# One step behind each chunk: splitting the attention rows inside a tuned streaming-encoder kernel

## The chip, the cores and the metric

The kernel runs on one core of a Trainium2 chip. The metric is device time in microseconds; a kernel's time is the median of several executions. One further execution was recorded by the hardware profiler, and every row of a profile in this text comes from such a recorded execution. The engines are TensorE (PE, with its weight loads listed apart as PEld), VectorE (DVE), ScalarE (ACT), GpSimd (POOL) and SyncE (SP), whose queue issues the transfers (DMA).

## The reference

The reference is one inference step of a one-layer hybrid encoder with 1024 prompt frames and 32 frames of a running stream. Two branches (gated linear attention and differential attention) each produce rows `y`, which are normalised, gated and projected; the two projections are gated again, added, projected by `w_out` and normalised.

```python
def out_merge(x, o_gla, o_diff, gg, dg, ma, mb, gla_norm_g, diff_subln_g, lambda_init,
              w_proj_gla, w_proj_diff, w_out, post_norm_g):
    yg = rmsnorm(o_gla, gla_norm_g).reshape(B, T, GLA_VAL) * jax.nn.silu(gg)
    yd = (rmsnorm(o_diff, diff_subln_g) * (1.0 - lambda_init)).reshape(B, T, DIFF_VAL) * jax.nn.silu(dg)
    merged = jax.nn.sigmoid(ma) * (yg @ w_proj_gla) + jax.nn.sigmoid(mb) * (yd @ w_proj_diff)
    return x + rmsnorm(merged @ w_out, post_norm_g)
```

All is float32. The kernel holds each matrix as a high part, rounded for TensorE, and a low part, what the rounding left; a product is three matmuls (high by high, low by high, high by low).

## The kernel before

The kernel goes through input projections with both attention branches interleaved, then the merge, which is what matters here. Everything is kept transposed: 8 tiles of 128 features by 1056 frames (1024 + 32). The merge has these parts:

1. **First product**, `yg @ w_proj_gla`, in 8 blocks j = 0 to 7 of 128 output features. Each block runs over 3 chunks of 352 frames, and each chunk is 8 x 3 = 24 matmuls into one PSUM bank (`ps_w`, L517 to L519; blocks 0 and 1 are written apart, L1172 to L1174). Two banks take turns. When a chunk is done, DVE evacuates it: one instruction multiplies it with the gate `tha` (L1155). After a block, `done()` stores the gated block to DRAM (`ptd`, L1188) and loads the gate of block j + 2 (L1151).
2. **Rows of the second kind**, `yd`. The 8 row tiles of the differential branch lie in DRAM without their rms scale. For each k: load the row (`ydr`, L1220; two buffers by parity of k), multiply it on DVE by its scale (L1229; the scales of a pair of rows lie in one tile `rsb`, broadcast to all partitions by a 1 MB load, L1225, one buffer), copy the high part on ACT (L1230) into `Y`, subtract on DVE to get the low part (L1231). Then the row buffer is free and row k + 2 is loaded. After an odd row the scale tile of the next pair is loaded.
3. **Second product**, `yd @ w_proj_diff`, with the same chunks and banks (L493 to L495). Its evacuation (L1250) gates a chunk with `thb`, then adds the stored first product `ptl` (L1251) and splits the sum into `m` (L1252 on ACT, L1253 on DVE).
4. **Output product** with `w_out`, whose 4 parts are loaded (`cwr`, L1262) and split as well (`cwh` on ACT, L1270; `cwl` on DVE, L1271). The first part uses the buffers that the rows had: `cwr` those of the even rows, `cwl` those of the odd ones, `cwh` that of the scale tiles.

For every block, the weights are loaded (`wr`, L481), rounded on ACT (`wh`, L483) and split on POOL (`wl`, L485) one block ahead.

In the stage of the change, PE and DVE run in the order in which the code is written (`manual_schedule`), so that DVE does nothing ahead of what stands before it. The orders of ACT and SP are made by a scheduler, and each engine keeps its own strictly. Row splitting stands in `done()` of blocks 3 to 7 (`BESIDE = range(3, KT)`, L40), hence behind all three evacuations of a block; `split_yd` does a whole row. Over blocks 3 to 7 it takes rows 0; 1, 2; 3; 4, 5; 6, 7.

Of the kernel before, what the change touches and what calls it, by code (L numbers as in the profile page):

```python
# [11 lines left out]
F32 = mybir.dt.float32  # L12
# [3 lines left out]
ALU = mybir.AluOpType  # L16
# [9 lines left out]
KT = D // P  # L26
# [13 lines left out]
BESIDE = range(3, KT)  # L40
# [90 lines left out]
def hybrid_step_kernel(ctx: ExitStack, tc: tile.TileContext, a):  # L131
# [3 lines left out]
    ve = nc.vector  # L135
# [3 lines left out]
    def pool(name, bufs=1, **kw):  # L139
        return tc.alloc_tile_pool(name=name, bufs=bufs, **kw)  # L140
# [20 lines left out]
    def bank(name):  # L161
        return bank_of("pj", name)
# [316 lines left out]
    def wtile(b):  # L479
        wr = wp.tile([P, KT, P], F32, tag="wr", bufs=1, name="wr")  # L480
        dma(wr, a["w128"][b])  # L481
        wh = odd(wp, KT, P, tag="wh", name="wh")
        act(wh, wr, AF.Copy)  # L483
        wl = odd(wp, KT, P, tag="wl", name="wl")
        nc.gpsimd.tensor_tensor(wl, wr, wh.bitcast(F32), op=ALU.subtract)  # L485
        return wh, wl
# [11 lines left out]
    def fill(jobs, src, then=None):  # L498

        w = wtile(jobs[0][0])  # L500
        for ji, (b, event, begin, needs) in enumerate(jobs):
            wh, wl = w
            evac = done = None
            for t0, n in CHUNKS:
                ps = None
                for k in range(KT):
                    if k % N["fill"] == 0:
                        yield 0.45 * N["fill"], (needs if ps is None else []), (["pj"] if ps is None else [])
                        if evac is None:
                            if ji + 1 < len(jobs):  # L510
                                w = wtile(jobs[ji + 1][0])
                            elif then is not None:
                                ahead.append(wtile(then))
                            evac, done = begin()
                        if ps is None:
                            ps = bank("ps_w")
                    mm(ps[:, :n], wh[:, k, :], src[k][:, 0, t0 : t0 + n], start=(k == 0), stop=False)  # L517
                    mm(ps[:, :n], wl[:, k, :], src[k][:, 0, t0 : t0 + n], start=False, stop=False)  # L518
                    mm(ps[:, :n], wh[:, k, :], src[k][:, 1, t0 : t0 + n], start=False, stop=(k == KT - 1))  # L519
                with tc.high_priority(offset=N["evac"]):  # L520
                    evac(ps[:, :n], slice(t0, t0 + n))
                S.free("pj", W["w_pj"])
            done()
            S.mark(event)

    ahead = []

    def silu_into(dst):

# [291 lines left out]
    with tc.manual_schedule(engines=PE):  # L821
        left = S.run([[gla_thread(), None, first], [prep_thread(), None, nullcontext],
                      [fill(jobs, xs), None, nullcontext]],
                     until=lambda: ("on", GH - 1, 1) in S.at and jobs[-1][1] in S.at)
# [306 lines left out]
    with tc.manual_schedule(engines=PE):  # L1131
        left = S.run(left + [[diff_main(), None, first], [sample_thread(), None, nullcontext],
                             [fill(jobs, xs, BLK_PG), None, nullcontext]],
                     until=lambda: ("pv", DH - 1, 3) in S.at and jobs[-1][1] in S.at)
# [13 lines left out]
    def load_tha(j):  # L1148
        if j < KT:
            tha[j] = ld("tha")  # L1150
            dma(tha[j], thd[0, j])  # L1151

    def pg_evac(j):
        def evac(ps, sl):
            ve.scalar_tensor_tensor(tha[j][:, sl], tha[j][:, sl], 1.0, ps, op0=ALU.add, op1=ALU.mult)  # L1155
        return evac

    def pg_first():

        w = [ahead.pop(), wtile(BLK_PG + 1)]  # L1160
        for j in range(2):
            load_tha(j)
        b = []
        for j, k in sorted(((j, k) for j in range(2) for k in range(KT)), key=lambda e: (e[1] + N["lead"] * e[0], e[0])):
            yield 1.36, [(("qk", DH - 1), W["yg0"] + W["yg"] * k)], [] if b else ["pj", "pj", "s", "s"]
            if not b:
                d = [dbank("ps_w") for _ in range(2)]
                b = [bank("ps_w"), bank("ps_w")] + [d[n // 2][:, n % 2 * 512 : n % 2 * 512 + 512] for n in range(4)]
            wh, wl = w[j]
            for n, (t0, cw) in enumerate(CHUNKS):  # L1170
                ps = b[j * 3 + n]
                mm(ps[:, :cw], wh[:, k, :], ytiles[k][:, 0, t0 : t0 + cw], start=(k == 0), stop=False)  # L1172
                mm(ps[:, :cw], wl[:, k, :], ytiles[k][:, 0, t0 : t0 + cw], start=False, stop=False)
                mm(ps[:, :cw], wh[:, k, :], ytiles[k][:, 1, t0 : t0 + cw], start=False, stop=(k == KT - 1))  # L1174
            if k == KT - 1:
                with tc.high_priority(offset=N["evac"]):
                    for n, (t0, cw) in enumerate(CHUNKS):
                        pg_evac(j)(b[j * 3 + n][:, :cw], slice(t0, t0 + cw))
                st(ptd[j], tha[j])
                load_tha(j + 2)  # L1180
                for tag in ("pj", "pj") if j == 0 else ("s", "s"):
                    S.free(tag, W["pg_b"])
        yield from fill([pg_job(j) for j in range(2, KT)], ytiles)

    def pg_job(j):
        def begin():
            def done():
                st(ptd[j], tha[j])  # L1188
                load_tha(j + 2)
                if j >= BESIDE[0]:  # L1190
                    for k in range(KT * (j - BESIDE[0]) // len(BESIDE), KT * (j + 1 - BESIDE[0]) // len(BESIDE)):
                        split_yd(k)
            return pg_evac(j), done
        return BLK_PG + j, ("pg", j), begin, []

# [9 lines left out]
    yd = [Y[k // 6][:, k % 6] for k in range(KT)]  # L1205
# [9 lines left out]
    rsb, ydr = {}, {}  # L1215

    def load_yd(k):
        if k < KT:
            ydr[k] = cp.tile([P, T], F32, tag=("cwr", "cwl")[k % 2], name="ydr")
            dma(ydr[k], ydd[k])  # L1220

    def load_rsb(k):
        if k < KT:
            rsb[k // 2] = cp.tile([P, 2, NP], F32, tag="cwh", name="rsb")
            dma(rsb[k // 2], rsd[k : k + 2, :].unsqueeze(0).to_broadcast([P, 2, NP]))  # L1225

    def split_yd(k):
        r = ydr[k]
        ve.tensor_tensor(r[:, 0:NP], r[:, 0:NP], rsb[k // 2][:, k % 2], op=ALU.mult)  # L1229
        act(yd[k][:, 0, :], r, AF.Copy)  # L1230
        ve.tensor_tensor(yd[k][:, 1, :], r, yd[k][:, 0, :].bitcast(F32), op=ALU.subtract)  # L1231
        if k % 2:
            load_rsb(k + 1)
        load_yd(k + 2)

    load_rsb(0)
    load_yd(0)
# [4 lines left out]
    for j in range(KT):  # L1242
# [6 lines left out]
        def evac(ps, sl, th=th, pt=pt, y=y):  # L1249
            ve.scalar_tensor_tensor(th[:, sl], th[:, sl], 1.0, ps, op0=ALU.add, op1=ALU.mult)  # L1250
            ve.tensor_tensor(pt[:, sl], pt[:, sl], th[:, sl], op=ALU.add)  # L1251
            act(y[:, 0, sl], pt[:, sl], AF.Copy, scale=0.5)  # L1252
            ve.scalar_tensor_tensor(y[:, 1, sl], pt[:, sl], 0.5, y[:, 0, sl].bitcast(F32), op0=ALU.mult, op1=ALU.subtract)  # L1253
# [20 lines left out]
    op = pool("op", reuse_waits="tile")  # L1274
# [51 lines left out]
    for u in range(4):  # L1326
# [5 lines left out]
        else:  # L1332

            raw = []
            for k in (0, 4):
                r = op.tile([P, D], F32, tag="xn", bufs=3, name="raw")
                r = r.rearrange("p (k n) -> p k n", k=4)
# [107 lines left out]
```

## Time and profile before

| what | us |
|---|---|
| median of the timed executions (3, from 1445.06 to 1446.31) | 1445.84 |
| profiled execution | 1439.49 |
| its span, first to last instruction | 1437.7 |
| TensorE busy in the span | 1394.2 |
| DVE busy in the span | 717.0 |

Busy time on TensorE is read with care: matmuls overlap, so a row's duration (0.32 us for 352 columns) is longer than the distance between two starts, and the distance between starts is what counts. In rows in order of time, the first number is the start in us from the beginning of the span, the second the duration; the bracket gives how long the engine was idle before and what ended that.

### The profile page before, as it was taken

Reading aid. Unit: us, or ns where it says so; the run is one execution under the profiler, and the core shown is the slowest. Engines: PE = TensorE matmul, PEld = TensorE weight load, DVE = VectorE, ACT = ScalarE, POOL = GpSimd, SP = SyncE. Lnnn points to the kernel's source line nnn. Section 1 sums busy time; section 2 is a strip of 40 time slices with the busy share of each in tenths; the row PEclk is TensorE's granted clock in tenths of the full one; section 3 lists DMA queues with packets and bytes.
Section 4 is the critical chain, followed back from the end, with each engine's and each line's share of the span. In section 5 each row is a group of like instructions: output and inputs, shape, how many; then the busy total and the mean of one; then the engine's idle time right before and its main releaser. Section 6 shows DMA issues by size and latency. Waiting matters only on the chain.

```text
span 1437.7 us, 22643 instructions
## 1 busy us (share of the span) xinstructions
PE 1394.2 (97%) x9074; PEld 1288.8 (90%) x9074; DVE 717.0 (50%) x1448; ACT 556.6 (39%) x1164; POOL 299.9 (21%) x194
## 2 busy tenths in 40 slices
PE   8999999999999999999999999999999999999997
PEld 7687789889989899998989898989999899899997
DVE  5522005666555342565655555565565424555425
ACT  4523104535344232454444444454554422221321
POOL 1200002222223223222232222222221122122002
PEclk9999999999999999999999999999999999999999
DMA  8422111122222233112221322122232475643434
GB/s 308 163 103 98 46 44 57 44 75 85 84 71 76 74 122 100 61 64 87 72 78 52 92 66 86 54 93 66 78 94 76 146 263 203 242 166 128 161 114 150
DMA packets 65251, 152.42 MB, mean 106 GB/s; under 512 B 9664, under 2 KB 28512, under 8 KB 63728
## 3 DMA queue, kind: packets, MB, share of 16 engines
q1 hardware_dynamic: 64992, 150.60, 31.5%
q8 instruction: 75, 1.23, 0.4%
q14 instruction: 40, 0.33, 0.1%
q10 hardware_dynamic: 144, 0.26, 0.0%
HBM read 108.60 MB, written 40.08 MB: 103 GB/s over the span
## 4 chain that ended last, share of the span: by engine, by line
PE 58%; DVE 5%; ACT 1%; issue 1%; DMA 0%; POOLq 0%; DVEq 0%; ACTq 0%
PE ps_w L517 11%; PE ps_w L518 11%; PE ps_w L519 11%; PE ps_s L944 4%; PE ps_t L1006 2%; PE ps_c L1291 2%; PE ps_c L1293 2%; PE ps_c L1292 2%; PE ps_w L495 2%; PE ps_w L493 2%; PE ps_w L494 2%; PE po L1020 1%; PE po L1021 1%; DVE nm L948 1%; PE po L1019 1%
## 5 line engine op out<-in xcount | busy, mean ns | idle before, releaser
L517 PE MATMUL ps_w<-X,wh 128*128 128x352 f32 x1344 | 449.9, 335 | 0.7 <-ACT vo L308 0.4
L518 PE MATMUL ps_w<-X,wl 128*128 128x352 f32 x1344 | 435.2, 324 | 0.8 <-issue 0.8
L519 PE MATMUL ps_w<-X,wh 128*128 128x352 f32 x1344 | 433.5, 323 | 0.0
L485 POOL TENSOR_TENSOR wl<-wr,wh 128x1024 fp32r<-128x1024 f32 x72 | 177.7, 2469 | 561.8 <-ACT wh L483 497.5
L517 PEld LDWEIGHTS ps_w<-X,wh 128*128 128x128 f32 x1344 | 252.8, 188 | 8.4 <-issue 4.7
L518 PEld LDWEIGHTS ps_w<-X,wl 128*128 128x128 f32 x1344 | 253.2, 188 | 1.1 <-issue 1.1
L519 PEld LDWEIGHTS ps_w<-X,wh 128*128 128x128 f32 x1344 | 252.5, 188 | 0.0
L950 ACT ACTIVATE p<-ps_s,nm 128x256 f32<-128x256 f32 (+7 forms) x128 | 94.5, 740 | 63.0 <-DVE nm L948 60.7
L483 ACT ACTIVATE wh<-wr 128x1024 fp32r<-128x1024 f32 x72 | 76.1, 1056 | 68.0 <-PE ps_w L519 40.8
L328 PE MATMUL ps_v<-wh,X 128*128 128x512 f32 x248 | 98.7, 398 | 0.0
L329 PE MATMUL ps_v<-wh,X 128*128 128x512 f32 x248 | 97.6, 394 | 0.8 <-DVE X L245 0.8
L330 PE MATMUL ps_v<-wl,X 128*128 128x512 f32 x248 | 98.3, 396 | 0.0
L948 DVE TENSOR_REDUCE nm<-ps_s 128x1 f32<-128x256 f32 (+7 forms) x128 | 93.2, 753 | 0.0
L1009 DVE TENSOR_TENSOR al<-ps_t,ah 128x512 fp32r<-128x512 f32 (+2 forms) x96 | 53.2, 554 | 35.6 <-ACT ah L1008 34.3
L1008 ACT ACTIVATE ah<-ps_t 128x512 fp32r<-128x512 f32 (+2 forms) x96 | 47.0, 489 | 60.8 <-PE ps_t L1006 60.3
L495 PE MATMUL ps_w<-Y,wh 128*128 128x352 f32 x192 | 61.9, 324 | 0.8 <-DVE Y L1231 0.7
L493 PE MATMUL ps_w<-Y,wh 128*128 128x352 f32 x192 | 62.0, 324 | 0.5 <-DVE thb L1250 0.5
L494 PE MATMUL ps_w<-Y,wl 128*128 128x352 f32 x192 | 61.8, 324 | 0.0
L308 ACT ACTIVATE vo<-ps_v 128x512 f32<-128x512 f32 x32 | 19.0, 595 | 105.7 <-PE ps_v L330 105.3
L1024 DVE SCALAR_TENSOR_TENSOR osb<-po,gs_half,sg 128x256 f32<-128x256 f32 x32 | 15.5, 483 | 88.3 <-ACT sqo L1023 88.3
L328 PEld LDWEIGHTS ps_v<-wh,X 128*128 128x128 f32 x248 | 46.7, 188 | 12.7 <-issue 1.7
L329 PEld LDWEIGHTS ps_v<-wh,X 128*128 128x128 f32 x248 | 46.7, 188 | 12.5 <-DVE X L245 1.7
(319 smaller groups left out, 2681.1 us busy)
## 6 DMA issues: line engine op xcount, KB each, us to landing
wr<-w SPq DMA_DIRECT2D x72, 512.0 KB
thd<-gate SPq DMA_DIRECT2D x16, 528.0 KB
wr<-wv SPq DMA_DIRECT2D x16, 512.0 KB
xn<-xn SPq DMA_DIRECT2D x12, 512.0 KB
newk<-pair SPq DMA_DIRECT2D x8, 528.0 KB
y<-ygd SPq DMA_DIRECT2D x8, 528.0 KB
tha<-thd SPq DMA_DIRECT2D x8, 528.0 KB
ydr<-ydd SPq DMA_DIRECT2D x8, 528.0 KB
```

The costliest lines, as they stand in the source:

```text
L328: mm(ps, xk[:, 0, t0 : t0 + P], wh[:, k, :], start=(k == 0), stop=False)
L329: mm(ps, xk[:, 1, t0 : t0 + P], wh[:, k, :], start=False, stop=False)
L330: mm(ps, xk[:, 0, t0 : t0 + P], wl[:, k, :], start=False, stop=(k == KT - 1))
L485: nc.gpsimd.tensor_tensor(wl, wr, wh.bitcast(F32), op=ALU.subtract)
L493: mm(ps[:, :n], wh[:, k, :], src[k][:, 0, t0 : t0 + n], start=(k == 0), stop=False)
L494: mm(ps[:, :n], wl[:, k, :], src[k][:, 0, t0 : t0 + n], start=False, stop=False)
L495: mm(ps[:, :n], wh[:, k, :], src[k][:, 1, t0 : t0 + n], start=False, stop=(k == KT - 1))
L517: mm(ps[:, :n], wh[:, k, :], src[k][:, 0, t0 : t0 + n], start=(k == 0), stop=False)
L518: mm(ps[:, :n], wl[:, k, :], src[k][:, 0, t0 : t0 + n], start=False, stop=False)
L519: mm(ps[:, :n], wh[:, k, :], src[k][:, 1, t0 : t0 + n], start=False, stop=(k == KT - 1))
L948: ve.tensor_reduce(nm, ps[:, 0:w], axis=AX.X, op=ALU.max, negate=True)
L950: act(p[:, 0:w], ps[:, 0:w], AF.Exp, bias=nm, accum_out=sums[m])
```

## The change

The row splitting is cut into single steps and moved. `scale_yd(k)` does the DVE multiplication and the ACT copy, and after an odd row the load of the next scale tile. `split_yd(k)` does the DVE subtraction and the load of row k + 2. A list of 15 steps is made: scale 0, split 0, scale 1, split 1, and so on, the fourteenth step holds split 6 and scale 7, the fifteenth split 7. A table `beside` hangs one step on each chunk of blocks 3 to 7, directly behind its evacuation.

```diff
                 S.free("pj", W["w_pj"])
+                if event in beside:
+                    beside[event]()
             done()
             S.mark(event)
 
-    ahead = []
+    ahead, beside = [], {}
...
                 load_tha(j + 2)
-                if j >= BESIDE[0]:
-                    for k in range(KT * (j - BESIDE[0]) // len(BESIDE), KT * (j + 1 - BESIDE[0]) // len(BESIDE)):
-                        split_yd(k)
...
-    def split_yd(k):
+    def scale_yd(k):
         r = ydr[k]
         ve.tensor_tensor(r[:, 0:NP], r[:, 0:NP], rsb[k // 2][:, k % 2], op=ALU.mult)
         act(yd[k][:, 0, :], r, AF.Copy)
-        ve.tensor_tensor(yd[k][:, 1, :], r, yd[k][:, 0, :].bitcast(F32), op=ALU.subtract)
         if k % 2:
             load_rsb(k + 1)
+
+    def split_yd(k):
+        ve.tensor_tensor(yd[k][:, 1, :], ydr[k], yd[k][:, 0, :].bitcast(F32), op=ALU.subtract)
         load_yd(k + 2)
+
+    steps = [f for k in range(KT - 1) for f in ((scale_yd, k), (split_yd, k))]
+    steps = [[f] for f in steps[:-1]] + [[steps[-1], (scale_yd, KT - 1)], [(split_yd, KT - 1)]]
+
+    def beside_chunk():
+        for f, k in steps.pop(0):
+            f(k)
+    beside.update({("pg", j): beside_chunk for j in BESIDE})
```

The changed file has other line numbers: the evacuation is L1157, the scaling L1228, the copy L1229, the split L1234; the loads of rows, scale tiles and gates are L1219, L1224 and L1153, the store L1190.

The order of the instructions on DVE, from the first product's evacuations on (`tha<-tha,ps_w`), before:

```order
L1155 SCALAR_TENSOR_TENSOR tha<-tha,ps_w 128x352 x12
L1229 TENSOR_TENSOR ydr<-ydr,rsb 128x1024
L1231 TENSOR_TENSOR Y_12709<-ydr,Y_12709 128x1056
L1155 SCALAR_TENSOR_TENSOR tha<-tha,ps_w 128x352 x3
L1229 TENSOR_TENSOR ydr<-ydr,rsb 128x1024
L1231 TENSOR_TENSOR Y_12709<-ydr,Y_12709 128x1056
L1229 TENSOR_TENSOR ydr<-ydr,rsb 128x1024
L1231 TENSOR_TENSOR Y_12709<-ydr,Y_12709 128x1056
L1155 SCALAR_TENSOR_TENSOR tha<-tha,ps_w 128x352 x3
```

and in the changed kernel at the same place:

```order
L1157 SCALAR_TENSOR_TENSOR tha<-tha,ps_w 128x352 x10
L1228 TENSOR_TENSOR ydr<-ydr,rsb 128x1024
L1157 SCALAR_TENSOR_TENSOR tha<-tha,ps_w 128x352
L1234 TENSOR_TENSOR Y_12709<-ydr,Y_12709 128x1056
L1157 SCALAR_TENSOR_TENSOR tha<-tha,ps_w 128x352
```

The first scaling moves from behind the twelfth evacuation to behind the tenth, and no two steps on rows stand next to each other; the alternation of the last four rows goes on to the end of block 7.

DVE at the end of block 7 and the beginning of the second product (`thb<-thb,ps_w`), before:

```order
L1155 SCALAR_TENSOR_TENSOR tha<-tha,ps_w 128x352 x3
L1229 TENSOR_TENSOR ydr<-ydr,rsb 128x1024
L1231 TENSOR_TENSOR Y_12710<-ydr,Y_12710 128x1056
L1229 TENSOR_TENSOR ydr<-ydr,rsb 128x1024
L1231 TENSOR_TENSOR Y_12710<-ydr,Y_12710 128x1056
L1250 SCALAR_TENSOR_TENSOR thb<-thb,ps_w 128x352 x2
L1251 TENSOR_TENSOR ptl<-ptl,thb 128x352 x2
L1253 SCALAR_TENSOR_TENSOR m_13198<-ptl,m_13198 128x352 x2
L1271 TENSOR_TENSOR cwl<-cwr,cwh 128x512 x3
```

and in the changed kernel:

```order
L1234 TENSOR_TENSOR Y_12710<-ydr,Y_12710 128x1056
L1228 TENSOR_TENSOR ydr<-ydr,rsb 128x1024
L1157 SCALAR_TENSOR_TENSOR tha<-tha,ps_w 128x352
L1234 TENSOR_TENSOR Y_12710<-ydr,Y_12710 128x1056
L1282 TENSOR_TENSOR cwl<-cwr,cwh 128x512
L1261 SCALAR_TENSOR_TENSOR thb<-thb,ps_w 128x352
L1282 TENSOR_TENSOR cwl<-cwr,cwh 128x512
L1262 TENSOR_TENSOR ptl<-ptl,thb 128x352
L1282 TENSOR_TENSOR cwl<-cwr,cwh 128x512
L1264 SCALAR_TENSOR_TENSOR m_13198<-ptl,m_13198 128x352
```

Only the split of row 7 is left behind the last evacuation of block 7. The splitting of the output weights (`cwl`) now begins ahead of the first evacuation of the second product; before, it stood behind the second.

The order of SP's transfers around the second and third scale tile (`rsb`), before:

```order
L1220 DMA ydr<-ydd 128x1056
L1188 DMA ptd<-tha 128x1056
L1225 DMA rsb<-rsd 128x2048
L1220 DMA ydr<-ydd 128x1056
L1151 DMA tha<-thd 128x1056
L481 DMA wr<-w 128x1024
L1220 DMA ydr<-ydd 128x1056
L1188 DMA ptd<-tha 128x1056
L1225 DMA rsb<-rsd 128x2048
```

and in the changed kernel:

```order
L1190 DMA ptd<-tha 128x1056
L1224 DMA rsb<-rsd 128x2048
L1153 DMA tha<-thd 128x1056
L1219 DMA ydr<-ydd 128x1056
L481 DMA wr<-w 128x1024
L1190 DMA ptd<-tha 128x1056
L1219 DMA ydr<-ydd 128x1056
L481 DMA wr<-w 128x1024
L1153 DMA tha<-thd 128x1056
L1224 DMA rsb<-rsd 128x2048
```

A row load and the weight load `wr` have changed places in block 4, and the third scale tile now follows a weight load and a gate load where it followed a row load and a store.

## The prediction

> **What bounds the kernel now.** I read the page first, then busy time by stage, then the waits of TensorE, then the rows of VectorE (DVE) in order of time around those waits.
>
> ```profile
> PE 1394.2 (97%) x9074; PEld 1288.8 (90%) x9074; DVE 717.0 (50%) x1448; ACT 556.6 (39%) x1164; POOL 299.9 (21%) x194
> ```
>
> TensorE is busy for 97% of the span, so a change can gain only where TensorE stands still or runs slow. The stage the change touches is projection blocks 3 to 7 of the first merge product and the start of the second. By windows (columns: stretch, its length, busy us of PE, PEld, DVE, ACT and POOL with counts, clock, DMA share, GB/s):
>
> ```profile
> 1167.00:1178.60 11.60, 11.60 (x74) 11.60 (x73) 2.00 (x4) 1.06 (x1) 2.43 (x1) 1.00 0.88 289
> 1178.60:1190.20 11.60, 11.60 (x75) 11.60 (x74) 1.56 (x3) 1.06 (x1) 2.40 (x1) 1.00 0.49 170
> 1190.20:1201.80 11.60, 11.60 (x74) 11.60 (x74) 4.86 (x5) 2.15 (x2) 2.77 (x1) 1.00 0.52 186
> 1201.80:1218.00 16.20, 13.16 (x74) 12.87 (x73) 7.23 (x7) 3.24 (x3) 2.73 (x1) 0.89 0.66 231
> 1218.00:1229.60 11.60, 11.60 (x74) 11.60 (x74) 4.86 (x5) 2.15 (x2) 2.77 (x1) 1.00 0.75 277
> 1229.60:1243.00 13.40, 11.89 (x74) 11.60 (x74) 7.25 (x7) 3.24 (x3) 2.40 (x1) 1.00 0.68 247
> 1243.00:1257.00 14.00, 12.75 (x75) 11.59 (x74) 10.78 (x14) 6.37 (x9) 2.77 (x1) 1.00 0.57 222
> 1257.00:1268.40 11.40, 11.40 (x73) 11.40 (x72) 6.54 (x11) 2.49 (x4) 2.77 (x1) 1.00 0.62 234
> ```
>
> A block of 72 matmuls takes 11.6 us when nothing disturbs it (the first three rows are blocks 2, 3 and 4). Blocks 5 and 7 (16.20 and 13.40) take longer with TensorE idle, and so does the start of the second product (14.00); behind it TensorE is full again (last row). In block 5 the clock also falls to 0.89. The DVE rows say why:
>
> ```profile
> 1182.65 0.52 DVE L1155 SCALAR_TENSOR_TENSOR tha<-tha,ps_w 128x352 f32<-128x352 f32 x1 [3.32 <-PE ps_w L519]
> 1190.37 0.52 DVE L1155 SCALAR_TENSOR_TENSOR tha<-tha,ps_w 128x352 f32<-128x352 f32 x1 [3.33 <-PE ps_w L519]
> ...
> 1201.97 0.52 DVE L1155 SCALAR_TENSOR_TENSOR tha<-tha,ps_w 128x352 f32<-128x352 f32 x1 [3.35 <-PE ps_w L519]
> 1202.41 1.22 DVE L1229 TENSOR_TENSOR ydr<-ydr,rsb 128x1024 f32<-128x1024 f32 x1
> 1204.78 2.23 DVE L1231 TENSOR_TENSOR Y<-ydr,Y 128x1056 fp32r<-128x1056 f32 x1 [1.16 <-ACT Y L1230]
> 1208.56 1.23 DVE L1229 TENSOR_TENSOR ydr<-ydr,rsb 128x1024 f32<-128x1024 f32 x1 [1.55 <-DMA rsb<-rsd]
> 1210.93 1.26 DVE L1231 TENSOR_TENSOR Y<-ydr,Y 128x1056 fp32r<-128x1056 f32 x1 [1.15 <-ACT Y L1230]
> 1212.11 0.95 DVE L1155 SCALAR_TENSOR_TENSOR tha<-tha,ps_w 128x352 f32<-128x352 f32 x2
> ...
> 1237.21 1.26 DVE L1231 TENSOR_TENSOR Y<-ydr,Y 128x1056 fp32r<-128x1056 f32 x1 [1.15 <-ACT Y L1230]
> 1238.39 0.95 DVE L1155 SCALAR_TENSOR_TENSOR tha<-tha,ps_w 128x352 f32<-128x352 f32 x2
> 1243.12 0.52 DVE L1155 SCALAR_TENSOR_TENSOR tha<-tha,ps_w 128x352 f32<-128x352 f32 x1 [3.78 <-PE ps_w L519]
> ...
> 1250.47 1.26 DVE L1231 TENSOR_TENSOR Y<-ydr,Y 128x1056 fp32r<-128x1056 f32 x1 [1.15 <-ACT Y L1230]
> ...
> 1264.70 0.52 DVE L1250 SCALAR_TENSOR_TENSOR thb<-thb,ps_w 128x352 f32<-128x352 f32 x1 [2.95 <-PE ps_w L495]
> ```
>
> The first two rows evacuate chunks 0 and 2 of block 3: 7.72 us for two chunks, 3.86 us each. Number the 15 chunks of blocks 3 to 7 from 0, and let e(i) be when evacuation i would start undisturbed: e(i) = 1182.65 + 3.86 i. After chunk 5 (1201.97) DVE runs two whole rows back to back, waits in the middle for a new scale tile, and comes to evacuate chunk 6 only at 1212.11, where e(6) = 1205.81. There are two banks for these chunks, so chunk 8 can't start before it:
>
> ```profile
> 1209.32 0.32 PE L519 MATMUL ps_w<-y,wh 128*128 128x352 f32 x1
> 1212.67 0.66 PE L517 MATMUL ps_w<-y,wh 128*128 128x352 f32 x1 [3.04 <-DVE tha L1155]
> 1213.14 0.49 PE L518 MATMUL ps_w<-y,wl 128*128 128x352 f32 x1
> ...
> 1215.73 0.32 PE L518 MATMUL ps_w<-y,wl 128*128 128x352 f32 x1
> ...
> 1237.13 0.32 PE L519 MATMUL ps_w<-y,wh 128*128 128x352 f32 x1
> 1238.96 0.43 PE L517 MATMUL ps_w<-y,wh 128*128 128x352 f32 x1 [1.51 <-DVE tha L1155]
> ```
>
> **The loss, summed.** Matmuls start every 3.86/24 = 0.161 us. The first stop costs 1212.67 - 1209.32 - 0.16 = 3.19. Then ten intervals up to 1215.73 take 3.06 instead of 1.61: 1.45 lost to the lower clock. The stop after chunk 11 costs 1.83 - 0.16 = 1.67 and 0.1 at its restart. Together 6.4. The evacuations confirm it: chunk 14 starts at 1243.12 against e(14) = 1236.69, 6.43 late. The start of the second product loses more: its fifth evacuation (1264.70) is e(19) = 1255.99, so 8.71 late in all, 2.28 of it new. That is where rows 6 and 7 are split only after chunk 14; the last split starts at 1250.47, while the first chunks of the product already want it.
>
> **The change part by part.** No arithmetic is added or taken away: 8 scalings, 8 copies, 8 splits stay. They are spread as one DVE step behind each of the 15 evacuations, and the first comes two chunks earlier.
>
> DVE's load per chunk: an evacuation holds DVE 0.44 (1202.41 - 1201.97), a scaling 1.22, a split 1.26, or 2.23 when it runs beside POOL's work on the next weights, as the rows above show for both. The ScalarE copy, for which a split waited 1.16 each time, now lies in the remainder of the chunk before. A chunk thus holds DVE for 1.7 to 2.7 of 3.86 us. The fullest is chunk 13 (split 6 and scaling 7): 0.44 + 1.26 + 1.22 = 2.9, at most 3.9 beside POOL. Evacuation i may start 3.3 late before TensorE feels it, since chunk i+2 starts at about e(i+1). No stop remains in blocks 3 to 7: gain 6.4. If the cover (the idle DVE of each chunk) were gone, the price would be the late microseconds beyond 3.3.
>
> What must arrive in time are transfers, since each load is issued behind a step and the SyncE (SP) queue is in order:
>
> ```profile
> 1203.65 4.88 DMA rsb<-rsd
> ```
> ```profile
> 1202.52 0.32 SPq L1188 DMA_DIRECT2D ptd<-tha  x1
> 1203.65 0.32 SPq L1225 DMA_DIRECT2D rsb<-rsd  x1
> ...
> 1247.10 0.33 SPq L481 DMA_DIRECT2D wr<-w  x1
> 1247.48 0.42 SPq L1244 DMA_DIRECT2D thb<-thd  x1
> 1248.21 10.39 SPq L1262 DMA_DIRECT2D cwr<-wout  x2
> ```
>
> A scale tile (1 MB) landed 4.88 us after issue, with a store of 528 KB issued 1.1 us ahead. Now it is issued after an odd scaling at e(2n) + 1.7 and wanted two chunks later at e(2n+2) + 0.44, 6.4 us on: hidden, with 1.5 to spare. The third scale tile has a weight load and a gate load just ahead of it (the order of SP, above) in place of a row load and a store, which may take up much of that. If late, DVE may wait 5.5 us more before TensorE does (scaling, 0.44 of evacuation and a hand-over before e(i+2)), so TensorE is safe to 11.9 us. Lower bound of the loss here 0, upper bound 1: I take 0. A row tile (528 KB) has 9.3 us between its issue and its use, row 7 at least 6.7. The weight loads now stand behind row loads that wait for a split, up to 2.7 us later than before; those weights are only needed a block (11.6) after ScalarE could take them, of which its 1.06 and POOL's 2.4 to 2.8 are used. DMA as a whole: the windows of blocks 3 to 7 move about 14.4 MB in 64.4 us, 223 GB/s; in 58 us it is 248, below the 289 of the quiet first window.
>
> At the second product split 7 follows evacuation 14 at e(14) + 0.44 and ends by e(14) + 2.7; its first use is the last matmuls of chunk 15, at about e(14) + 3.4. So the 2.28 goes too. But the DVE order now puts the first split of the output weights (cwl) ahead of the first evacuation there. It waits for ScalarE's copy, and that for a 1 MB load (cwr):
>
> ```profile
> 1254.64 2.20 ACT L1270 ACTIVATE cwh<-cwr 128x512 fp32r<-128x512 f32 x4
> ```
> ```profile
> SPq L1262 <- DMA cwr<-wout: 6.0, 1, 6.0
> ```
>
> The load landed at about 1248.5 + 6.0 = 1254.5, 6.3 after its issue, with two loads (1.04 MB) just ahead. Now it is issued when split 6 ends, e(13) + 1.7, which is e(14) - 2.2, with the queue idle. By the row it lands by e(14) + 4.1; a copy piece (0.55) and a cwl piece (0.6) bring the evacuation to about e(14) + 5.3 instead of 3.86; it must be done by e(16) = e(14) + 7.72. TensorE loses nothing if the load lands within 8.2 us. Between 0 and, at double the row's 6.3, 4.4 I take 0, which is nearest to the row.
>
> Sum: 6.43 + 2.28 = 8.7 off the profiled span of 1437.7, which becomes 1429.0 (executed: 1439.49 to 1430.8). The timed runs have a median of 1445.84, 6.3 above the profiled execution; the stops are a matter of order, so I take the same 8.7 off it: **1437.1**.
>
> [...] The row: after a stop of 3.3 us ten matmuls took 3.06 instead of 1.61 us. [...]
>
> **Rivals.**
> 1. *The slow stretch is not in every timed run.* [...] For it: the stop of 1.7 us after chunk 11 brought no slow stretch. Against: the same code stops the same way each time.
> 2. *A new wait in place of the old*: the output weights' load comes later than 8.2 us after its issue and holds the first evacuation of the second product. For: DVE is strictly in order and this load is new ahead of an evacuation. Against: 6.3 measured in fuller traffic. A landing 9.5 to 11 us after issue gives 1.3 to 2.8, and 1.45 if the clock falls: around 1440.
> 3. *The gain is absorbed later.* For: DVE waited for a load in the second product (row below), so that stage could be bound by transfers. Against: the wait is 0.25, and the window after 1257.00 shows TensorE full. Then 0 is left: 1445.8.
>
> ```profile
> 1273.23 0.53 DVE L1251 TENSOR_TENSOR ptl<-ptl,thb 128x352 f32<-128x352 f32 x1 [0.25 <-DMA ptl<-ptd]
> ```
>
> 4. *Slower: the scale tiles starve.* One chain: a scaling issues the next scale tile, which is wanted two chunks on, behind a weight and a gate load. It decides beyond 11.9 us from issue to landing, and then on all three tiles: at 15 us, 3 x (3.1 + 1.45) = 13.7, so 1450.8. Against: 4.88 measured, and 289 GB/s was carried for a whole block.
> 5. *It doesn't do what it says*: another wait keeps the evacuations late, and only the stop on the scale tile goes, 3.19 + 1.45: 1441.2. The order of DVE shows one step behind each evacuation, so hardly.
>
> **How the numbers follow.** Forecast 0.66, rival 1 0.10, rival 2 0.12, rival 3 0.06, rival 4 0.04, rival 5 0.02. About 0.2% (2.9 us) is what a measurement of this kernel tells from no change. Forecast and rivals 1, 2 and 5 are faster, 0.90; rival 3 is the same, 0.06; rival 4 slower, 0.04. The range: downwards, a second slow stretch of 1.45 in the timed runs of the kernel before and their spread of 0.6 make a gain of 10.7, 1435.1; upwards, rival 1 and most of rival 2: 1441.0.
>
> **What would show it.** Right: evacuations of blocks 3 to 7 every 3.86 us to the end, chunk 14 near 1236.7; no wait of TensorE for tha (it was 3.0 and 1.5); clock 1.00 in each block; splits that no longer wait 1.16 for ScalarE; the fifth evacuation of the second product near 1256.0. Wrong: a DVE wait on rsb or ydr over 5 us, a wait of TensorE at chunk 17 with DVE behind cwl, or the same end time with new idle time after 1260.

## The result, and the profile after

The changed kernel's median is 1434.11 us (six executions, 1432.50 to 1436.39) against 1445.45 for the kernel before (six, 1441.33 to 1448.39). The ratio is 0.9932, with a 95% interval from 0.9916 to 0.9949: 9.8 us faster, between 7.4 and 12.1. The forecast was 8.7 off and 1437.1. The median itself lies 1.0 below the low end of the range (1435.1); the ratio applied to the 1445.84 of the prediction gives 1436.0, inside it.

By windows, blocks 3 to 7 and the first block of the second product in the changed kernel (columns as in the prediction):

```profile
1181.00:1192.60 11.60, 11.60 (x74) 11.60 (x73) 3.87 (x5) 2.15 (x2) 2.40 (x1) 1.00 0.49 163
1192.60:1204.20 11.60, 11.60 (x74) 11.60 (x73) 5.00 (x6) 3.24 (x3) 2.77 (x1) 1.00 0.83 297
1204.20:1215.80 11.60, 11.60 (x74) 11.60 (x73) 5.10 (x6) 2.15 (x2) 2.39 (x1) 1.00 0.76 279
1215.80:1227.40 11.60, 11.60 (x74) 11.60 (x73) 7.36 (x6) 3.24 (x3) 2.44 (x1) 1.00 0.76 254
1227.40:1239.00 11.60, 11.60 (x74) 11.60 (x73) 6.17 (x7) 3.10 (x3) 2.75 (x1) 1.00 0.81 271
1239.00:1250.60 11.60, 11.60 (x75) 11.60 (x73) 7.03 (x12) 4.35 (x8) 2.79 (x1) 1.00 0.80 272
```

TensorE is full in each, the clock is 1.00 in each. The DVE rows, with the first, tenth, eleventh and fifteenth evacuation of the stage (L1157) and the first and fifth evacuation of the second product (L1261):

```profile
1185.00 0.52 DVE L1157 SCALAR_TENSOR_TENSOR tha<-tha,ps_w 128x352 f32<-128x352 f32 x1 [3.32 <-PE ps_w L519]
...
1217.10 3.50 DVE L1228 TENSOR_TENSOR ydr<-ydr,rsb 128x1024 f32<-128x1024 f32 x1 [0.69 <-DMA rsb<-rsd]
1220.51 0.51 DVE L1157 SCALAR_TENSOR_TENSOR tha<-tha,ps_w 128x352 f32<-128x352 f32 x1
1221.75 1.26 DVE L1234 TENSOR_TENSOR Y<-ydr,Y 128x1056 fp32r<-128x1056 f32 x1 [0.73 <-ACT Y L1229]
1223.61 0.52 DVE L1157 SCALAR_TENSOR_TENSOR tha<-tha,ps_w 128x352 f32<-128x352 f32 x1 [0.61 <-PE ps_w L519]
...
1239.04 0.52 DVE L1157 SCALAR_TENSOR_TENSOR tha<-tha,ps_w 128x352 f32<-128x352 f32 x1 [1.03 <-PE ps_w L519]
1239.48 1.25 DVE L1234 TENSOR_TENSOR Y<-ydr,Y 128x1056 fp32r<-128x1056 f32 x1
1243.20 0.69 DVE L1282 TENSOR_TENSOR cwl<-cwr,cwh 128x512 fp32r<-128x512 f32 x1 [2.47 <-ACT cwh L1281]
1243.81 0.52 DVE L1261 SCALAR_TENSOR_TENSOR thb<-thb,ps_w 128x352 f32<-128x352 f32 x1
...
1258.35 0.52 DVE L1261 SCALAR_TENSOR_TENSOR thb<-thb,ps_w 128x352 f32<-128x352 f32 x1 [1.39 <-PE ps_w L495]
```

From the first evacuation of block 3 to the fifth of the second product are 1258.35 - 1185.00 = 73.35 us; before they were 1264.70 - 1182.65 = 82.05. The difference is 8.70. What is behind it takes 1431.4 - 1258.35 = 173.05, before 1437.7 - 1264.70 = 173.00. But the span fell by 6.3 only, from 1437.7 to 1431.4, because in this execution the stage began 2.35 later; up to there both kernels have the same orders, and 2.2 of it arose in the first 90 us. The stage's beginning moved between 1182.65 and 1187.73 over the thirteen profiles of this case, whatever the kernel. So the stage is measured from its own start in what follows; that tells a tenth of a microsecond, where two spans tell a few.

### The profile page after: what moved, and what is told of

Its sections match the earlier page's. It is cut to its first block, busy times and chain, and to the rows that moved or that the text cites. A ratio compares the mean times of both kernels' runs of the same rounds, so it can differ in the third digit from the quotient of the medians.

```text
span 1431.4 us, 22644 instructions
## 1 busy us (share of the span) xinstructions
PE 1392.7 (97%) x9074; PEld 1288.6 (90%) x9074; DVE 715.0 (50%) x1448; ACT 556.6 (39%) x1164; POOL 299.4 (21%) x194
## 4 chain that ended last, share of the span: by engine, by line
PE 60%; DVE 4%; ACT 1%; issue 1%; POOLq 0%; DVEq 0%; ACTq 0%
PE ps_w L517 11%; PE ps_w L518 11%; PE ps_w L519 11%; PE ps_s L946 4%; PE ps_t L1008 2%; PE ps_w L494 2%; PE ps_w L493 2%; PE ps_w L495 2%; PE ps_c L1302 2%; PE ps_c L1304 2%; PE ps_c L1303 2%; PE po L1022 1%; PE po L1023 1%; DVE nm L950 1%; PE po L1021 1%; PE ps_w L1174 1%
```

## The experiments

Columns: from evacuation 0 to 14 (blocks 3 to 7); from evacuation 0 to 19 (the fifth of the second product); from there to the end of the span; ratio of the timed executions to the kernel before, where there are enough.

| kernel | 0 to 14 | 0 to 19 | behind | ratio (95% interval) |
|---|---|---|---|---|
| before | 60.47 | 82.05 | 173.0 | 1 |
| before, again | 62.48 | 84.05 | 173.0 | |
| before, third | 60.35 | 81.95 | 173.1 | |
| changed | 54.04 | 73.35 | 173.1 | 0.9932 (0.9916 to 0.9949) |
| changed, again | 54.05 | 73.36 | 173.1 | |
| whole rows behind every second chunk | 54.20 | 74.57 | 173.1 | 0.9944 (0.9927 to 0.9961) |
| single steps, two chunks later | 54.05 | 76.31 | 173.1 | 0.9961 (0.9946 to 0.9975) |
| before, scale tile in halves | 57.35 | 78.95 | 176.2 | 0.9982 (0.9966 to 0.9998) |
| the same, again | 57.36 | 78.95 | 172.8 | |
| changed, scale load written later | 54.05 | 73.55 | 173.0 | 0.9932 (0.9914 to 0.9950) |
| changed, scale tile in halves | 54.05 | 73.35 | 173.1 | 0.9929 (0.9913 to 0.9946) |
| changed, scale tile held to the split | 57.51 | 76.81 | 173.9 | |
| changed, scale tile held to its use | 63.31 | 83.16 | 171.5 | |

**The kernel before, twice more, and the changed kernel once more.** No edit.

> The kernel before, unchanged, profiled once more. Theory (the stops follow from the order of DVE): from the first evacuation of block 3 to the fifth of the second product again 82.05 us within 0.5, of which 8.7 is loss. Rival (the slow stretch of the clock comes and goes): 80.6 without it, or 83.5 with a second one. What lies before block 3 may differ from the first profile by a few us in either direction; that is not the stage's.

> The kernel before, unchanged, a third profile, on the chip of the runs sent with it. As for the second: 82.05 us within 0.5 for the stage, or 80.6 to 83.5 if the slow stretch of the clock comes and goes.

> The changed kernel, profiled once more. Theory (nothing stops TensorE in the stage any more, so nothing is left there to vary): 73.35 us within 0.1 from the first evacuation of block 3 to the fifth of the second product, and 173.05 behind it. Rival (the stage of the changed kernel varies as that of the kernel before does, 82.0 to 84.1): over 73.8.

The third profile repeats the first, 81.95. The second takes 84.05. Its rows of TensorE around the stop in block 7, between chunks 13 and 14, and the window of that block:

```profile
1240.03 0.32 PE L519 MATMUL ps_w<-y,wh 128*128 128x352 f32 x1
1242.18 0.43 PE L517 MATMUL ps_w<-y,wh 128*128 128x352 f32 x1 [1.83 <-DVE tha L1155]
...
1243.25 0.45 PE L517 MATMUL ps_w<-y,wh 128*128 128x352 f32 x1
...
1246.43 0.46 PE L519 MATMUL ps_w<-y,wh 128*128 128x352 f32 x1
1246.72 0.33 PE L517 MATMUL ps_w<-y,wh 128*128 128x352 f32 x1
```
```profile
1232.80:1247.80 15.00, 13.17 (x72) 12.88 (x72) 7.37 (x7) 3.13 (x3) 2.40 (x1) 0.89 0.70 249
```

Here the stop in block 7 was 2.15 - 0.16 = 2.0 long, and from 1.1 us after the restart the matmuls started every 0.29 us up to 1246.72: a second slow stretch, clock 0.89. So the kernel before loses 8.6 to 10.7 in this stage from one execution to the next, measured against the changed kernel's 73.35, and the changed kernel, which doesn't stop, repeats to 0.01 in its two profiles (a third one with the same orders, below, takes 0.2 more).

**Whole rows behind every second chunk.** The single steps are undone; the spread stays.

```diff
-    steps = [f for k in range(KT - 1) for f in ((scale_yd, k), (split_yd, k))]
-    steps = [[f] for f in steps[:-1]] + [[steps[-1], (scale_yd, KT - 1)], [(split_yd, KT - 1)]]
+    steps = [[(scale_yd, n // 2), (split_yd, n // 2)] if n % 2 == 0 else [] for n in range(3 * len(BESIDE))]
```

> The changed kernel, but with a whole row (scaling, copy, split) behind every second chunk in place of one step behind each. Theory (two banks forgive 3.3 us, and what cost time was two rows in a row and the wait for a scale tile): blocks 3 to 7 lose nothing, 54.04 us from the first to the fifteenth evacuation as in the changed kernel; the last row ends 4.1 to 5.1 us after the fifteenth evacuation, where it is wanted after 3.4, so 0.7 to 1.7 is lost at the second product: 74.1 to 75.1 us to its fifth evacuation (changed kernel 73.35). Rival (the single steps are what counts, because a whole row with its wait for ScalarE holds DVE longer than a chunk): 4.1 to 5.1 against 3.86, up to 1.2 lost for each of 8 rows, up to 83 us.

```profile
1241.48 0.52 DVE L1157 SCALAR_TENSOR_TENSOR tha<-tha,ps_w 128x352 f32<-128x352 f32 x1 [2.08 <-PE ps_w L519]
1241.92 1.22 DVE L1228 TENSOR_TENSOR ydr<-ydr,rsb 128x1024 f32<-128x1024 f32 x1
1244.29 2.25 DVE L1234 TENSOR_TENSOR Y<-ydr,Y 128x1056 fp32r<-128x1056 f32 x1 [1.16 <-ACT Y L1229]
```

Blocks 3 to 7 lose 0.15 in all; a row that holds DVE longer than a chunk (4.99 us against 3.86, from the evacuation at 1195.00 to the next) is forgiven by the two banks here, where a chunk without a row follows. The last row ends 5.06 after the last evacuation (1246.54 - 1241.48), and the second product loses 1.06, so that row was wanted about 4.0 after that evacuation, not the 3.4 that the prediction had. Of the 8.7, spreading whole rows alone brings 7.5 (82.05 - 74.57); cutting them into steps brings the last 1.2, nearly all at the one place where row 7's scaling and copy then lie ahead of the last evacuation.

**Single steps, two chunks later.** Rows 6 and 7 stay whole behind the last chunk.

```diff
-    steps = [f for k in range(KT - 1) for f in ((scale_yd, k), (split_yd, k))]
-    steps = [[f] for f in steps[:-1]] + [[steps[-1], (scale_yd, KT - 1)], [(split_yd, KT - 1)]]
+    steps = [(f, k) for k in range(KT) for f in (scale_yd, split_yd)]
+    steps = [[], []] + [[f] for f in steps[:12]] + [steps[12:]]
```

> The changed kernel's single steps, begun two chunks later, so that rows 6 and 7 are done whole behind the last chunk of block 7, as before the change. Theory: blocks 3 to 7 lose nothing (54.04 us), and the start of the second product loses the 2.28 it lost before: 75.6 us to the fifth evacuation. Rival (the second product's start lost time because everything was late): 73.4.

```profile
1239.88 0.52 DVE L1157 SCALAR_TENSOR_TENSOR tha<-tha,ps_w 128x352 f32<-128x352 f32 x1 [2.16 <-PE ps_w L519]
1240.96 1.23 DVE L1228 TENSOR_TENSOR ydr<-ydr,rsb 128x1024 f32<-128x1024 f32 x1 [0.56 <-DMA rsb<-rsd]
...
1247.88 1.26 DVE L1234 TENSOR_TENSOR Y<-ydr,Y 128x1056 fp32r<-128x1056 f32 x1 [1.15 <-ACT Y L1229]
```

Blocks 3 to 7 are clean (54.05), and the second product's start loses 2.96 (76.31 against 73.35), where theory had 2.28 and its rival nothing. The 0.7 above theory is nearly all in the first of these waits, 0.56 for a scale tile that now comes late as well. So the second term of the sum belongs to rows 6 and 7, not to lateness earlier on.

**The kernel before, with the scale tile in halves.** Place and grouping of the rows stay; each half of the tile is loaded as soon as its row is scaled.

```diff
+    rsb2 = cp.tile([P, 2, NP], F32, tag="cwh", name="rsb")
     def load_rsb(k):
         if k < KT:
-            rsb[k // 2] = cp.tile([P, 2, NP], F32, tag="cwh", name="rsb")
-            dma(rsb[k // 2], rsd[k : k + 2, :].unsqueeze(0).to_broadcast([P, 2, NP]))
+            dma(rsb2[:, k % 2 : k % 2 + 1], rsd[k : k + 1, :].unsqueeze(0).to_broadcast([P, 1, NP]))
...
-        if k % 2:
-            load_rsb(k + 1)
+        load_rsb(k + 2)
...
     load_rsb(0)
+    load_rsb(1)
```

> The kernel before, with the scale tile loaded in two halves, each as soon as its own row is scaled, so that no row waits for its scales; grouping and place of the rows stay. Theory: the stop in block 5 shrinks to that of block 7 (1.8 us) and the slow clock behind it goes: 57.6 us to the fifteenth evacuation (before 60.47), 79.9 to the fifth of the second product (before 82.05). Rival (the scale tile is all that stops block 5): 55.8 and 78.1. Other rival (the wait for scales was hidden anyway): 60.5 and 82.

> The kernel before with half scale tiles, profiled once more, for what lay behind the stage: 176.2 us there in its first profile against 173.0 in the other kernels. If the order of the kernel makes it, 176.2 again; if it was that one execution, 173.0. The stage itself: 78.95 within 0.2 again.

Its TensorE waits over the stage, in the first of its two profiles (columns: who waited for whom, us, times, longest):

```profile
PE ps_w L517 <- DVE tha L1155: 2.8, 2, 1.4
PE ps_w L495 <- DVE Y L1232: 0.7, 1, 0.7
PE ps_w L493 <- DVE thb L1251: 0.5, 1, 0.5
```

Blocks 5 and 7 now stop alike, 1.4 of waiting each, and without a slow stretch: 57.35. So of the 6.43 in the blocks, 3.1 were the scale tile with the clock behind it, and 3.3 the two rows in a row. To the fifth evacuation of the second product theory had 79.9; that was added up wrongly, 57.6 with the 21.6 of before gives 79.2, and 78.95 was measured. What lay behind the stage took 176.2 in one profile and 172.8 in the other: that was one execution, with matmuls from about 1360 us on starting every 0.119 instead of 0.113 us, and its cause is open.

**The scale load written later.** The load of the next scale tile was moved from `scale_yd` to the end of `split_yd`.

> The changed kernel, with each scale tile loaded one chunk later: behind the split of the odd row in place of its scaling, so that 2.6 us are left between issue and use where a load took 4.9 to 7. Theory (TensorE forgives a scaling that is up to 5.5 us late): DVE waits 2 to 5 us for each of three tiles, and TensorE loses nothing, or up to 1.3 where POOL's work falls on the late scaling: 73.4 to 74.7 us from the first evacuation of block 3 to the fifth of the second product (changed kernel 73.35). Rival (the supply of scales has no room): each wait is felt, three times 2.7 or more, 81 us.

```profile
1194.22 0.32 SPq L1224 DMA_DIRECT2D rsb<-rsd  x1
...
1236.72 0.33 SPq L1273 DMA_DIRECT2D cwr<-wout  x1
```
```profile
1245.29 0.69 DVE L1282 TENSOR_TENSOR cwl<-cwr,cwh 128x512 fp32r<-128x512 f32 x1 [4.74 <-ACT cwh L1281]
1245.90 0.52 DVE L1261 SCALAR_TENSOR_TENSOR thb<-thb,ps_w 128x352 f32<-128x352 f32 x1
```

This shows nothing on the question. The stage began at 1184.81, so the load was issued 1.7 after evacuation 2, as in the changed kernel, and the orders of DVE, ScalarE, POOL and SP's transfers came out as the changed kernel's; that the scheduler put the load back where its buffer came free is inferred from that. 73.55 lies in the range of theory, but not for its reason. So this run is a third profile of the changed kernel's orders. Its 0.2 more arose in one place: the output weights landed 7.9 after their issue (ScalarE took them up at 1244.62), and the first evacuation of the second product began 7.04 after evacuation 14 (1238.86) and so 3.18 late. The wait for scales had to be made by a use of the tile, as in the next two.

**The scale tile held to the split, and to its use.** A one-column copy (an addition, its result unused) reads the tile late, and the load follows it.

```diff
+    hold = cst.tile([P, 1], F32, name="hold")
...
     def split_yd(k):
         ve.tensor_tensor(yd[k][:, 1, :], ydr[k], yd[k][:, 0, :].bitcast(F32), op=ALU.subtract)
+        if k % 2:
+            ve.tensor_copy(hold, rsb[k // 2][:, 1, 0:1])
+            load_rsb(k + 1)
         load_yd(k + 2)
```

In the second kernel the copy and the load stand at the head of `scale_yd(k)` for k = 2, 4, 6.

> The changed kernel, with each scale tile held until the split of its odd row: a one-column DVE copy (an addition, its result unused) reads the tile there, and the load follows it, so that 2.6 us are left between issue and use where a load took 4.9 to 7. Theory (an evacuation may start 3.3 us late before TensorE stands): DVE waits 2 to 5 us for each of three tiles, TensorE loses nothing, 73.4 us for the stage, or up to 1.3 more where POOL's work falls on a late scaling. Rival (the supply of scales has no room): each wait is felt, three times 2.7 or more, 81 us.

> As the one before, but the one-column copy and the load of the scale tile stand right ahead of the scaling that needs it, so that DVE waits for the whole load. Theory, with L from issue to landing: the next evacuation starts 0.5 + L + 1.3 after this one against 3.86, and TensorE loses what lies beyond 3.3, that is L - 5.4 for each of three tiles: nothing at L = 4.9, 1.8 at 7.2, and 1.4 more where a stop is long enough for the clock to fall. The stage then takes 73.4 to 80 us, as L comes out. Rival (DVE's waits count in full): three times L - 2, 82 to 89 us.

The first kernel's loads and scalings of the second scale tile on, and its TensorE stops:

```profile
1198.56 0.42 SPq L1224 DMA_DIRECT2D rsb<-rsd  x1
1215.68 0.37 SPq L1224 DMA_DIRECT2D rsb<-rsd  x1
1232.62 0.32 SPq L1224 DMA_DIRECT2D rsb<-rsd  x1
```
```profile
1206.71 2.13 DVE L1230 TENSOR_TENSOR ydr<-ydr,rsb 128x1024 f32<-128x1024 f32 x1 [5.88 <-DMA rsb<-rsd]
...
1224.91 1.23 DVE L1230 TENSOR_TENSOR ydr<-ydr,rsb 128x1024 f32<-128x1024 f32 x1 [7.04 <-DMA rsb<-rsd]
...
1237.47 1.23 DVE L1230 TENSOR_TENSOR ydr<-ydr,rsb 128x1024 f32<-128x1024 f32 x1 [2.31 <-DMA rsb<-rsd]
```
```profile
1209.33 0.43 PE L517 MATMUL ps_w<-y,wh 128*128 128x352 f32 x1 [1.35 <-DVE tha L1157]
...
1226.62 0.43 PE L517 MATMUL ps_w<-y,wh 128*128 128x352 f32 x1 [1.58 <-DVE tha L1157]
```

DVE waited 5.88, 7.04 and 2.31; TensorE lost 1.6, 1.85 and nothing, together the 3.46 by which the stage is longer (behind it 0.9 more, whose cause is open). The forgiveness is real, and about 3.1 us for an evacuation, not 3.3: evacuation 5 began at 1208.76, 4.6 late, and the stop behind it was 1.67 - 0.16 = 1.5 long. Theory had 73.4 to 74.7, so 76.81 is a miss, and the size of the loads made it: they took 8.1, 9.2 and 4.8 from issue to landing, where 4.9 to 7 was assumed. The first two stood right behind a row load in the queue.

In the second kernel the loads took 7.2, 6.1 and 6.5, and the first two stops cost 2.1 and 1.35, where the L - 5.4 of theory gives 1.8 and 0.7. But the stage is 9.8 longer, of which 1.5 comes back behind it (171.5), where an evacuation and not TensorE was late. 83.16 lies above theory's 80 and in the range of its rival, 82 to 89; yet the rival's L - 2 gives 5.2, 4.1 and 4.5 for these loads, and no stop cost that much. TensorE's waits over the stage, and the rows around the third load:

```profile
PE ps_w L517 <- DVE tha L1157: 2.9, 2, 1.9
PE ps_w L493 <- ACT wh L483: 1.3, 1, 1.3
PE ps_w L493 <- DVE tha L1157: 1.1, 1, 1.1
PE ps_w L493 <- DVE thb L1264: 0.3, 1, 0.3
```
```profile
1244.44 0.51 DVE L1157 SCALAR_TENSOR_TENSOR tha<-tha,ps_w 128x352 f32<-128x352 f32 x1
1245.99 2.62 DVE L1237 TENSOR_TENSOR Y<-ydr,Y 128x1056 fp32r<-128x1056 f32 x1 [1.04 <-ACT Y L1234]
...
1249.67 0.51 DVE L1157 SCALAR_TENSOR_TENSOR tha<-tha,ps_w 128x352 f32<-128x352 f32 x1
```
```profile
1243.53 0.32 PE L519 MATMUL ps_w<-y,wh 128*128 128x352 f32 x1
1245.10 0.40 PE L493 MATMUL ps_w<-Y,wh 128*128 128x352 f32 x1 [1.25 <-ACT wh L483]
...
1248.66 0.43 PE L495 MATMUL ps_w<-Y,wh 128*128 128x352 f32 x1
1250.23 0.43 PE L493 MATMUL ps_w<-Y,wh 128*128 128x352 f32 x1 [1.13 <-DVE tha L1157]
```

The third stop was 1.57 - 0.16 = 1.41 long. The view names ScalarE's rounding of weights (`wh`) for it, because that ended last, at 1244.99. But the evacuation of chunk 13, which frees the bank, began 4.42 late and ended only at 1244.95, so the bank alone explains about 1.3. The rounded weights can't be those of the matmul that started: in the changed kernel TensorE began the second product at 1238.85 and ScalarE took up the same rounding after it, at 1239.09. What theory lacked came behind that stop. Split 6 and scaling 7 follow evacuation 13 together; ScalarE's copy for split 6 stood behind the rounding, and the split took 2.62 where the six ahead of it took 1.25 or 1.26; that POOL's split of the same weights ran beside it is inferred, from when the rounding ended. So evacuation 14 began 5.23 after evacuation 13 and stopped TensorE a fourth time, again for 1.41.

**The changed kernel with the scale tile in halves.** The same edit of `load_rsb`, on the changed kernel.

> The changed kernel with the scale tile loaded in two halves, each as soon as its own row is scaled. Theory: DVE's wait of 0.69 for a scale tile and the scaling of 3.50 us behind it go, every scaling takes 1.2 to 1.3, and TensorE gains nothing, since it lost nothing: 73.35 us for the stage, the same time as the changed kernel. Rival (late evacuations still cost something): 72.6 to 73.2 and a faster kernel.

```profile
L1229 DVE TENSOR_TENSOR ydr<-ydr,rsb x8: 1218/1220/1220, 1184.7 to 1236.1; 128x1024 f32<-128x1024 f32 x8
```

All eight scalings take 1.22 and none waits (shortest, median and longest in ns). The stage takes 73.35 and the ratio is the changed kernel's within its interval. 19 chunks of 3.86 are 73.34, so there is nothing left to gain in this stage by feeding DVE better.

## Why the prediction was right, point by point

*Stops in blocks 3 to 7, 6.43:* 60.47 - 54.04 = 6.43. (The stop that the prediction puts after chunk 11 lies between chunks 13 and 14; the two rows that cause it stand behind evacuation 11.) The cause is shown from both sides: taking the wait for the scale tile away from the kernel before brings 3.1, spreading the rows the rest.

*Start of the second product, 2.28:* 8.70 - 6.43 = 2.27, and it comes back when rows 6 and 7 are put behind the last chunk again, as 2.96 with one more late scale tile in it.

*The third scale tile would nearly use up its time:* it was issued at 1209.91 and landed when the scaling began at 1217.10, 7.2 instead of the 4.88 seen before, and DVE waited 0.69. So the 1.5 us to spare weren't there, and the zero taken for this load came true by the forgiveness behind it. The scaling then took 3.50 instead of 1.22, which no term had; the evacuation behind it was 0.8 late (1220.51 against 1185.00 + 9 x 3.86 = 1219.74). Both cost TensorE nothing, as the 3.3 of forgiveness said; its size is nearer 3.1. The split behind that scaling still waited 0.73 for ScalarE, against the sign that none would; no other split of the stage waited.

```profile
1209.91 0.32 SPq L1224 DMA_DIRECT2D rsb<-rsd  x1
...
1236.91 0.33 SPq L1273 DMA_DIRECT2D cwr<-wout  x1
```

*A new wait ahead of the second product (rival 2):* it is there, and cost nothing. DVE waited 2.47 for ScalarE's copy of the output weights, whose load (issued at 1236.91, second row above) landed 5.6 after its issue, and the first evacuation began 4.8 after evacuation 14 where 5.3 was worked out and about 7.2 allowed. In the run with the scale load written later, which has the same orders, the load took 7.9, the evacuation began at 7.04, and 0.2 was lost: the point of 8.2 was a little too late, as the forgiveness was too large.

*The clock (rival 1):* mis-sized, and towards the other side. The sum took one slow stretch of 1.45 as certain; the rival took it as absent from some timed runs, where 8.7 - 1.45 = 7.25 would be left. Three profiles show one in block 5 each time, and a second one in block 7 once, behind a stop of 2.15 us. With it the loss is 10.7, which is the low end's own reasoning come true. This fits the timed gain, 9.8, lying above the 8.7 of one pair of profiles; that the timed executions had it more often is argued, not shown, and the interval (7.4 to 12.1) holds 8.7 as well.

*The span, 1429.0:* 1431.4, because the part ahead of the stage took 2.35 more in that execution. The step that failed is to set the sum off one profiled span: the stage's own length was right to 0.01, the span wrong by 2.4.

*Rivals 3 and 5* fall with 173.05 behind the stage and the clean windows. *Rival 4*, the starving scale tiles, had a true mechanism and no occasion: with the load held to its use, stage and remainder together take 254.6 (83.16 + 171.48), as long as the kernel before (255.05), with loads of 6 to 7 us. Its point of decision, 11.9 us from issue to landing, was near the truth: counted from e(2n) + 1.7, where the load was to be issued, the tiles of that kernel began to cost at 11.7 to 11.8 (the first landed at about 1209.63, 13.85 after e(2) + 1.7 = 1195.78, and the stop was 2.02 long).

## What to carry to other kernels

With two banks taking turns, DVE could begin an evacuation about 3.1 us late here, of a chunk of 3.86, before TensorE stood. So work beside the evacuations cost nothing where a piece between two of them stayed below a chunk and that forgiveness (3.9 and 3.1 us) and the next chunk let DVE catch up; spread it evenly and early, and look at what is left behind the last chunk. Measure such a change from the stage's own first event, since what runs ahead of it moved by up to 5 us over the profiles here. A transfer that is issued behind a step is best counted from the step's place in the order to the use, with the slowest load of its size seen in that traffic, not the first one found.

## What the runs showed of the hardware

**A late scaling met POOL.** In the changed kernel POOL's weight split began 0.03 us before the scaling that took 3.50:

```profile
1217.07 2.44 POOL L485 TENSOR_TENSOR wl<-wr,wh 128x1024 fp32r<-128x1024 f32 x1 [8.27 <-ACT wh L483]
```

POOL was done at 1219.51 and the scaling at 1220.60, 1.09 later; the seven other scalings of the stage took 1.22 to 1.28, so this one did nearly nothing until POOL was done. Other rows agree, in both directions. Five of the eight splits in the kernel before began while POOL's split ran; they took 2.23 to 2.33 instead of 1.26, and each ended 1.1 us after POOL's (the one that began at 1204.78 ended at 1207.01, POOL's at 1205.89). In the changed kernel three steps of DVE began 0.75 ahead of POOL's split, at 1193.16, 1227.92 and 1239.48; they took 1.22 to 1.25, and POOL's split 2.75 to 2.79 instead of 2.40. Why the two engines hold each other up, no row shows.

**Slow matmuls behind stops.** In the three profiles of the kernel before, TensorE's stops in block 5, of 3.35, 3.28 and 3.15 us between two starts, were followed by matmuls that started every 0.29 instead of 0.16 us; the clock in the window of the block was 0.89 in the first two of these profiles. Of two stops of 2.15 and 2.18 us the first was followed by such matmuls (1240.03 to 1242.18, above) and the second, in the kernel with the scale tile held to its use (1209.16 to 1211.34), was not. Eleven stops between 1.40 and 1.90 were not. So in this stage slow matmuls followed the three stops of 3.15 and more and none of 1.90 and less, and the two between differ.
